# First four tiles of x and two units of weights as one sequence in a fixed order on each engine, with loads in parts and products of ones as TensorE's first work

## The chip, the cores and the metric

The kernel runs on one core of one Trainium2 chip. The metric is device microseconds from one launch to its end; where several executions were timed, the median counts. Each row of the profile comes from one profiled execution, whose own time and span are given below. The core has five engines that run their own instruction streams in order: TensorE (PE, with its weight loads shown apart as PEld), VectorE (DVE), ScalarE (ACT), GpSimd (POOL) and SyncE (SP). SP issues nearly all the DMAs here; in the rows, SPq is its queue.

## What is computed

One layer of an encoder trunk over x (2048 positions, 1024 channels, float32): RMSNorm, one input projection split into ten groups of 1024 columns, a gated linear recurrence in both directions (branch A), a spatial gating unit (branch B), two merge gates, an output projection and a final RMSNorm. Cut to its skeleton:

```python
h = _rmsnorm(x, norm_w[layer])
proj = jnp.einsum('bsd,de->bse', h, w_in[layer])
(q_raw, ffwd_raw, fbwd_raw, i_raw, ga_raw,
 u_raw, v_raw, gb_raw, ma_raw, mb_raw) = jnp.split(proj, split_points, axis=-1)
y_a = _hgrn2_branch(q_raw, ffwd_raw, fbwd_raw, i_raw, ga_raw, lb[layer, 0], lb[layer, 1], gnorm_w[layer])
y_b = _spatial_gating_branch(u_raw, v_raw, gb_raw, ln_w[layer], ln_b[layer], w_s[layer], b_s[layer])
merged = (jax.nn.sigmoid(ma_raw) * jnp.einsum('bsw,wd->bsd', y_a, w_proj_a[layer])
          + jax.nn.sigmoid(mb_raw) * jnp.einsum('bsw,wd->bsd', y_b, w_proj_b[layer]))
x = x + jnp.einsum('bsd,de->bse', merged, w_out[layer])
return _rmsnorm(x, final_norm_w)
```

Only the first line and the first two column groups used (i_raw, here called v, and q_raw) matter for the change.

## The kernel before

Every float32 operand of a projection is kept as two float16 parts, a high one and a low one, and each product is made of three matmuls into one PSUM tile: high by high, high by low, low by high (`mm3`, lines 211 to 218; the rows of lines 215, 216 and 217). The contraction of 1024 is eight steps of 128, so one output tile takes 24 matmuls.

**x.** The 2048 positions are 16 tiles of 128 rows, four to a segment `b`. `x_load` (line 260) fetches a tile of 512 KB into one of three buffers. `x_tile` (line 265) then does the following: ScalarE squares the tile and sums it (line 270); GpSimd makes the reciprocal root in two small instructions (lines 293, 294); for each half `i` of the channels VectorE multiplies by the root and by the norm weights `nwb[i]`, which were broadcast to all partitions by a DMA (line 275); TensorE transposes four blocks into PSUM (line 279); ScalarE writes the high part (line 280) and VectorE the low part (line 281) into `xT[b]`. The scale `sx` of x comes from `scale_x` (line 79): a small DMA of the norm weights, a maximum on VectorE, a transpose and a product on TensorE, and a power of two.

**Weights.** A unit is 1024 rows by 256 columns of `w_in`, 1024 KB. `halves` (line 170) loads it with one DMA (line 177), sums its squares in two pieces on ScalarE (line 182), converts the sums on GpSimd (line 185), adds them over the partitions with two small products on TensorE (line 191), makes a power of two from them (`pow2`, line 126, four VectorE instructions of one column, and line 196), writes the high part in two ScalarE instructions of 1024 columns (line 203) and the low part in one VectorE instruction of 2048 columns (line 204). `load` starts this and gives back a function that ends it; `unit` and `plan` keep the list of units: v, q, and the two forget gates for each pair of heads, 16 units in all, then two wide ones.

**Who decides the order.** A scheduler places the traced instructions on each engine; `tc.high_priority(40)` pulls a block ahead of what is traced before it. `hook(cols, f)` calls `f` in the trace once so many matmul columns have been traced, so that work for a later tile is traced inside the products of an earlier one.

**The start.** `phase1` (line 298) loads the first tile of x, calls `scale_x`, starts the first unit (v) at raised priority, fetches the two halves of `nwb`, and then loops over segments and tiles. After each second tile `v_seg` (line 427) makes v for two tiles of positions: 48 matmuls of 256 columns and one eviction on ScalarE (line 432). After the four tiles of a segment `q_seg` (line 435) makes q of one head: 24 matmuls of 512 columns, then a sigmoid on ScalarE (line 440, with a table load ahead of the first), a product on VectorE (line 444) and a sum of squares on ScalarE (line 445). After segment 3 come `decays` and the recurrence's loop, in which `gla_operands` (line 448), `gla_scores`, `gla_states` and `gla_outputs` work on segments of 512 positions while the projections of the next one run.

## Time and profile before

| what | value |
|---|---|
| median of three timed runs | 2392.24 us (2387.44 to 2392.54) |
| the profiled execution's own time | 2392.29 us |
| its span, first to last instruction | 2390.6 us |
| mean granted TensorE clock | 0.995 |
| TensorE busy | 2322.1 us (97%), 12880 matmuls |
| VectorE, ScalarE, GpSimd busy | 1541.3, 1019.9, 277.3 us |

A row of the timeline gives the start in us, the duration in us, the engine, the line, the operation, the tiles as out<-in with the shape, and how many equal instructions were merged; in brackets stands how long the engine sat idle before it and what released it. A row of the windows gives a stretch, its length, the busy time of TensorE with the number of matmuls, the granted clock, the share of DMA time and GB/s. A matmul's duration includes its way through the array, so in a stream the distance from start to start counts, not the duration. A row of the waits names who waited for whom, the sum in us, the number of times and the longest.

### The profile page before, as it was taken

Reading aid. Unit: us, or ns where it says so; the run is one execution under the profiler, and the core shown is the slowest. Engines: PE = TensorE matmul, PEld = TensorE weight load, DVE = VectorE, ACT = ScalarE, POOL = GpSimd, SP = SyncE. Lnnn points to the kernel's source line nnn. Section 1 sums busy time; section 2 is a strip of 40 time slices with the busy share of each in tenths; the row PEclk is TensorE's granted clock in tenths of the full one; section 3 lists DMA queues with packets and bytes.
Section 4 is the critical chain, followed back from the end, with each engine's and each line's share of the span. In section 5 each row is a group of like instructions: output and inputs, shape, how many; then the busy total and the mean of one; then the engine's idle time right before and its main releaser. Section 6 shows DMA issues by size and latency. Waiting matters only on the chain. (4 is left out here: it accounts for less than half of the span.)

```text
span 2390.6 us, 33841 instructions
## 1 busy us (share of the span) xinstructions
PE 2322.1 (97%) x12880; PEld 1295.7 (54%) x12880; DVE 1541.3 (64%) x3032; ACT 1019.9 (43%) x1870; POOL 277.3 (12%) x507
## 2 busy tenths in 40 slices
PE   7999999999999999999999999999999999999998
PEld 5666866685668566544554554444444444444443
DVE  5686648755773677696555556677665655577754
ACT  6524332433333334333445455656654533244432
POOL 2222202220212121211000000000000000000011
PEclk9999999999999999999999999999999999999999
DMA  5201110011001001122432223666665574777733
GB/s 178 79 6 31 36 36 10 27 36 36 14 23 52 2 14 58 47 62 80 133 101 84 83 86 141 225 248 253 234 219 184 191 274 160 269 238 272 251 117 115
DMA packets 169486, 281.26 MB, mean 118 GB/s; under 512 B 10976, under 2 KB 105184, under 8 KB 162144
## 3 DMA queue, kind: packets, MB, share of 16 engines
q1 hardware_dynamic: 169312, 278.98, 34.4%
q8 instruction: 104, 1.70, 0.3%
q14 instruction: 70, 0.57, 0.1%
HBM read 174.08 MB, written 104.86 MB: 117 GB/s over the span
## 5 line engine op out<-in xcount | busy, mean ns | idle before, releaser
L808 PEld LDWEIGHTS <-seven 128*128 128x128 f16 x5376 | 524.6, 98 | 641.2 <-issue 27.9
L808 PE MATMUL bank<-seven 128*128 128x512 f16 x2016 | 438.3, 379 | 9.1 <-DVE zs L822 7.1
L808 PE MATMUL bank<-xT,seven 128*128 128x512 f16 x1920 | 428.5, 381 | 4.8 <-ACT zs L775 2.4
L808 PE MATMUL bank<-xs,seven 128*128 128x512 f16 x1440 | 319.3, 379 | 0.0
L217 PE MATMUL pin<-xT,wsplit 128*128 128x512 f16 x768 | 291.2, 379 | 0.2 <-DVE wsplit L204 0.2
L215 PE MATMUL pin<-xT,wsplit 128*128 128x512 f16 x768 | 291.1, 379 | 0.2 <-ACT xT L280 0.2
L216 PE MATMUL pin<-xT,wsplit 128*128 128x512 f16 x768 | 291.1, 379 | 0.0
L216 PE MATMUL pin<-wsplit,xT 128*128 128x256 f16 (+1 forms) x768 | 238.2, 310 | 2.7 <-DVE wsplit L204 2.1
L217 PE MATMUL pin<-wsplit,xT 128*128 128x256 f16 (+1 forms) x768 | 238.3, 310 | 2.0 <-DVE xT L281 1.7
L215 PE MATMUL pin<-wsplit,xT 128*128 128x256 f16 (+1 forms) x768 | 238.0, 310 | 0.8 <-ACT xT L280 0.8
L822 DVE SCALAR_TENSOR_TENSOR zs<-bank,us,zs 128x512 f32<-128x512 f32 x120 | 88.9, 745 | 74.1 <-PE bank L808 72.8
L829 ACT ACTIVATE zs<-zs 128x512 f32<-128x512 f32 x120 | 75.2, 627 | 135.0 <-DVE zs L822 134.8
L217 PEld LDWEIGHTS <-wsplit 128*128 128x128 f16 x768 | 75.1, 98 | 90.3 <-DVE wsplit L204 0.7
L700 DVE TENSOR_TENSOR tmp<-raw 128x512 f32<-128x512 f32 x64 | 43.9, 689 | 124.0 <-ACT tmp L685 110.7
L822 DVE SCALAR_TENSOR_TENSOR zs<-bank,su,zs 128x512 f32<-128x512 f32 x72 | 53.8, 747 | 104.3 <-PE bank L808 80.3
L216 PEld LDWEIGHTS <-wsplit 128*128 128x128 f16 x768 | 75.1, 98 | 77.5
L215 PEld LDWEIGHTS <-wsplit 128*128 128x128 f16 x768 | 75.4, 98 | 75.8
L504 POOL TENSOR_TENSOR q<-ff,e 128x512 f32<-128x512 f32 x64 | 73.3, 1145 | 371.8 <-DVE e L502 213.4
L457 ACT ACTIVATE fz<-pin,wus 128x512 f32<-128x512 f32 x64 | 43.9, 685 | 144.3 <-PE pin L217 144.1
L775 ACT ACTIVATE zs<-bank,us 128x512 f32<-128x512 f32 x120 | 80.5, 677 | 50.6 <-PE bank L808 47.6
L217 PEld LDWEIGHTS <-xT 128*128 128x128 f16 x768 | 75.7, 99 | 42.1 <-DVE xT L281 4.6
L461 DVE TENSOR_SCALAR fz<-fz,fb,fa 128x512 f32<-128x512 f32 x64 | 35.6, 556 | 97.2 <-ACT fz L457 97.2
(205 smaller groups left out, 3618.5 us busy)
## 6 DMA issues: line engine op xcount, KB each, us to landing
kept<-seven SPq DMA_DIRECT2D x16, 1792.0 KB, 7.9
seven<-kept SPq DMA_DIRECT2D x16, 1792.0 KB, 9.2
wraw<-in_w_in_dram SPq DMA_DIRECT2D x20, 1024.0 KB, 5.1
raw<-in_w_in_dram SPq DMA_DIRECT2D x40, 512.0 KB, 4.8
xt<-in_x_dram SPq DMA_DIRECT2D x16, 512.0 KB, 4.1
o_d<-ob SPq DMA_DIRECT2D x32, 256.0 KB, 2.3
v<-V SPq DMA_DIRECT2D x16, 512.0 KB, 3.5
vl<-v SPq DMA_DIRECT2D x32, 256.0 KB, 2.9
```

The lines of the kernel that those rows point to most:

```text
L215: nc.tensor.matmul(ps, lh(k), rh(k), start=(k == 0), stop=False)
L216: nc.tensor.matmul(ps, lh(k), rl(k), start=False, stop=False)
L217: nc.tensor.matmul(ps, ll(k), rh(k), start=False, stop=(k == KT - 1))
L457: nc.scalar.activation(out=fz[:, 1:SEG + 1], in_=ps, func=AF.Sigmoid, scale=us)
L461: nc.vector.tensor_scalar(out=f, in0=f, scalar1=fb, scalar2=fa, op0=ALU.mult, op1=ALU.add)
L504: nc.gpsimd.tensor_tensor(out=q0.rearrange("p (m c) -> p m c", c=64), in0=ff.rearrange("p (m c) -> p m c", c=64), in1=e8.rearrange("p n b ...
L700: sub = lambda out, x, y: self.nc.vector.tensor_tensor(out=out, in0=x, in1=y, op=ALU.subtract)
L775: self.nc.scalar.activation(out=t, in_=ps, func=AF.Copy, scale=su)
L808: nc.tensor.matmul(ps, lhs(x, k), rhs(y, k), start=start and not (k or n), stop=k == 3 and n == 2, skip_group_check=True)
L822: self.nc.vector.scalar_tensor_tensor(out=more, in0=ps, scalar=su, in1=more, op0=ALU.mult, op1=ALU.add)
L829: self.nc.scalar.activation(out=out, in_=more, func=func)
```

## The change

`phase1` no longer treats segment 0 in its loop. A new method `start` writes out, as one sequence, everything up to v of all four tiles of segment 0, and the preparation of the q unit. Inside `in_order` each instruction gets an ordering edge to the one traced before it on the same engine, so each engine runs its part in exactly this order; a block `issue_after` puts what follows behind the last of them on each engine, until the constants of `phase1` have been traced.

In `start`:

- TensorE's first work is ten float32 products of `ones` by `ones` (128 by 128) into a PSUM tile that nobody reads; five more stand behind `scale_x`, three behind the first tile's transposes, six behind the sums of the weights' squares: 24 in all (`busy`).
- The first tile of x is the first DMA on SP's queue (before: the second, behind the v unit). The small load of the norm weights in `scale_x` goes to ScalarE's queue. The v unit comes in four DMAs of 256 KB (`part`), two behind each half of `nwb`; the loads of tiles 1, 2 and 3 follow, then the q unit.
- ScalarE squares the first tile of x, then the four parts of the unit. The low part of the unit is made in four VectorE instructions of 512 columns, the high part in four ScalarE instructions of 512 columns; the square of tile 1 stands ahead of the four high parts.
- The high part of the first tile's first half is written by VectorE (`alone=True`), all others by ScalarE.
- Squares, norms, transposes and splits of tiles 1 to 3 are hooked into the 96 products of v at fixed steps. The q unit is begun (`begin`) in the second tile's products and ended (`end`) in the third's.

Outside `start`: `x_tile` is divided into `x_rstd`, `x_norm`, `x_turn` and `x_split`; and `halves` makes the low part of every unit with `w_part`, in two VectorE instructions of half the columns, each behind its own half of the high part, where it was one instruction behind both.

```diff
@@ scale_x
-            nc.sync.dma_start(out=nwt, in_=self.nw.rearrange("(p k) -> p k", k=KT))
+            nc.scalar.dma_start(out=nwt, in_=self.nw.rearrange("(p k) -> p k", k=KT))
@@ halves
             for h in range(2):
-                ks = slice(h * K // 2, (h + 1) * K // 2)
-                nc.scalar.activation(out=wt[:, 0, ks], in_=raw[:, ks], func=AF.Copy, scale=s)
-            nc.vector.scalar_tensor_tensor(out=wt[:, 1].rearrange("p k n -> p (k n)"),
...
+                self.w_part(raw, wt, s, slice(h * K // 2, (h + 1) * K // 2))
+    def w_part(self, raw, wt, s, ks, which=(0, 1)):
+        flat = lambda z: z[:, ks].rearrange("p k n -> p (k n)")
+        if 0 in which:
+            self.nc.scalar.activation(out=wt[:, 0, ks], in_=raw[:, ks], func=AF.Copy, scale=s)
+        if 1 in which:
+            self.nc.vector.scalar_tensor_tensor(out=flat(wt[:, 1]), in0=flat(raw), scalar=s, in1=flat(wt[:, 0]),
+                                                op0=ALU.mult, op1=ALU.subtract)
+    @contextmanager
+    def in_order(self, last):
+        traced = self.nc.cur_bb.bb.instructions
+        old = traced[-1]
+        yield
+        start = next(n for n in reversed(range(len(traced))) if traced[n] is old) + 1
+        for ins in traced[start:]:
+            if ins.engine in last:
+                self.tc.add_manual_dep(ins, last[ins.engine].name, ...)
+            last[ins.engine] = ins
+    def start(self, nwb, last):
...
+            busy(10)
+            x = [self.x_load(0)]
+            self.scale_x()
+            busy(5)
+            for i in range(2):
+                t = self.gat.tile([P, SEG], F32, name="nwb", tag="at")
+                nc.sync.dma_start(out=t, in_=self.nw[i * SEG:(i + 1) * SEG].partition_broadcast(P))
+                nwb.append(t)
+                for ks in part[2 * i:2 * i + 2]:
+                    nc.sync.dma_start(out=raw[:, ks], in_=rows[:, ks])
+            x += [self.x_load(t) for t in range(1, 4)]
+            rstd = self.x_rstd(0, 0, x[0])
+            ss = [sm.tile([P, 2], F32, name="wss") for _ in range(2)]
+            for h, ks in enumerate(part):
+                nc.scalar.activation(out=wt[:, 1, ks], in_=raw[:, ks], func=AF.Square, accum_out=ss[h // 2][:, h % 2:h % 2 + 1])
+            sb = [sm.tile([P, 2], BF16, name="wsb") for _ in range(2)]
+            for h in range(2):
+                nc.gpsimd.tensor_copy(out=sb[h], in_=ss[h])
+            for i in range(2):
+                self.x_norm(x[0], rstd, nwb, i)
+            pt = [self.x_turn(0, i, x[0]) for i in range(2)]
+            busy(3)
+            self.x_split(0, 0, 0, pt[0], True)
+            pb = self.pg.tile([P, 1], F32, name="misc")
+            for h in range(4):
+                nc.tensor.matmul(pb, self.ones16, sb[h // 2][:, h % 2:h % 2 + 1], start=(h == 0), stop=(h == 3))
+            busy(6)
...
+            self.pow2(s, inv, pb)
...
+            self.x_split(0, 0, 1, pt[1])
+            rstd = {1: self.x_rstd(0, 1, x[1])}
+            wi, got = (wt, us), {}
+            for h in range(2):
+                self.w_part(raw, wt, s, part[h])
+            for h in range(2):
+                self.w_part(raw, wt, s, part[2 + h], (0,))
...
+            square(2)
+            for i in range(2):
+                norm(1, i)
+                self.w_part(raw, wt, s, part[2 + i], (1,))
+            for t, k, f in ((0, 4, partial(split, 1, 0)), (0, 6, partial(split, 1, 1)), (0, 6, partial(square, 3)),
+                            (0, 8, partial(norm, 2, 0)), (0, 8, partial(norm, 2, 1)),
+                            (1, 4, partial(split, 2, 0)), (1, 6, partial(split, 2, 1)), (1, 6, begin),
+                            (1, 8, partial(norm, 3, 0)), (1, 8, partial(norm, 3, 1)),
+                            (2, 4, partial(split, 3, 0)), (2, 6, partial(split, 3, 1)), (2, 7, end)):
+                self.hook((8 * t + k) * 3 * U, f)
+            v = self.v_seg(0, *wi, range(1))
+            v = self.v_seg(0, *wi, range(1, 2), v)
+        return wi, got["q"], v
@@ phase1
-                first = [self.x_load(0)]
-                self.scale_x()
-                with tc.high_priority(40):
-                    wi = self.load(*self.todo[0])
...
-                for b in range(NSEG):
+                last = {}
+                with tc.high_priority(60):
+                    wi, wq, vt[0] = self.start(nwb, last)
+                behind = ExitStack()
+                for ins in last.values():
+                    behind.enter_context(tc.issue_after(ins))
+                qs[0] = self.q_seg(0, 0, 0, *wq)
+                for b in range(1, NSEG):
                     for j in range(4):
-                        self.x_tile(b, j, nwb, first.pop() if first else self.x_load(4 * b + j))
-                        if j == 1 and b == 0:
...
-                        elif j % 2:
+                        self.x_tile(b, j, nwb, self.x_load(4 * b + j))
+                        if j % 2:
                             vt[b] = self.v_seg(b, *wi, range(j // 2, j // 2 + 1), vt[b])
```

As built, ScalarE's order around the q unit also differs. Before, it ran: the two squares of the third unit (a forget gate's), first eviction of v, high parts of tile 3, high parts of the q unit, squares of tiles 4, 5 and 6, second eviction of v, table load, sigmoid of q, high parts of tile 4. Now it runs: first eviction of v, high parts of tile 3, high parts of the q unit, second eviction of v, squares of tiles 4, 5 and 6, the two squares of the third unit, table load, sigmoid of q, high parts of tile 4. On SP's queue the third unit's load stands behind two more tiles of x than before. From the recurrence's loop on, the order on TensorE, ScalarE, GpSimd and SyncE is the same but for short runs of a few instructions that stand a few places earlier or later; VectorE has the second low half of each unit in addition.

## The prediction

> **What bounds the kernel now.** I read the page first, then TensorE by stretches, then the timeline of the first 40 us, then who waits for whom.

> ```profile
> span 2390.6 us, 33841 instructions
> PE 2322.1 (97%) x12880; PEld 1295.7 (54%) x12880; DVE 1541.3 (64%) x3032; ACT 1019.9 (43%) x1870; POOL 277.3 (12%) x507
> ```
> ```profile
> 0.00:14.00 14.00, 3.19 (x14) 1.00 0.87 289
> 14.00:31.00 17.00, 15.47 (x123) 1.00 0.62 196
> 31.00:60.00 29.00, 27.81 (x202) 1.00 0.34 114
> 60.00:105.00 45.00, 42.50 (x305) 0.96 0.23 80
> 105.00:960.00 855.00, 845.71 (x5601) 1.00 0.09 28
> ```

> TensorE sets the end: it is idle for 68.5 us of 2390.6. Of these, 10.8 lie before 14 us, 1.5 in 14 to 31, 1.2 in 31 to 60, 2.5 in 60 to 105 and 9.3 in 105 to 960. The change rewrites what happens before 31 us, so at most some 12 us of idle time are there to be had, 0.5% of the whole. Busy time hides a second loss:

> ```profile
> 13.87 0.39 PE L215 MATMUL pin<-wsplit,xT 128*128 128x256 f16 x1
> 15.50 0.37 PE L216 MATMUL pin<-wsplit,xT 128*128 128x256 f16 x1 [1.24 <-DVE wsplit L204]
> ...
> 16.36 0.42 PE L215 MATMUL pin<-wsplit,xT 128*128 128x256 f16 x1
> 16.57 0.42 PE L216 MATMUL pin<-wsplit,xT 128*128 128x256 f16 x1
> ...
> 20.35 0.27 PE L217 MATMUL pin<-wsplit,xT 128*128 128x256 f16 x1
> 20.46 0.27 PE L215 MATMUL pin<-wsplit,xT 128*128 128x256 f16 x1
> ```

> The first real matmul starts at 13.87 and the second at 15.50. At 16.4 two starts lie 0.21 apart, at 20.4 0.11: TensorE runs at half pace up to about 19.8, over some 17 matmuls, which costs 1.8 us. The clock also falls later:

> ```profile
> 67.60:71.00 3.40, 1.80 (x13) 1.00 0.60 239
> 71.00:74.40 3.40, 3.40 (x19) 0.50 0.00 0
> ```

> A stretch with 1.6 us idle of 3.4 is followed by 3.4 us at half clock, a loss of 1.7.

> **The change part by part.** *Loads.* These rows give the landings:

> ```profile
> 2.38 1.14 SPq L320 DMA_DIRECT2D nwb<-in_norm_w_dram  x2
> 6.51 1.06 ACT L182 ACTIVATE wsplit<-wraw 128x1024 f16<-128x1024 f32 x1 [4.44 <-DMA wraw<-in_w_in_dram]
> 7.98 0.16 DVE L88 TENSOR_REDUCE am<-nwt 128x1 f32<-128x8 f32 x1 [6.78 <-DMA nwt<-in_norm_w_dram]
> ```
> ```profile
> DMA to landing us min/median/max: 7.0/7.2/7.3
> ```

> The unit's 1024 KB land at 6.5; x's 512 KB and the tiny load behind them by 8.0. So 512 KB take 1.5, the unit 3.0, and data flow from 3.5. The last row is `nwb`'s: issued at 2.4 and 3.0, landed at 9.4 and 10.3, so 256 KB of broadcast take 0.9 to 1.4; I use 1.2. A quarter of a unit is bounded by half of an x tile, 0.75, and by a broadcast, 1.4; its rows are read once from memory as x's are, so 0.75. In the new order x lands at 5.0, the first `nwb` at 6.2, parts at 6.95 and 7.7, the second `nwb` at 8.9, parts at 9.65 and 10.4, tile 1 at 11.9. The tiny load, first on ScalarE's queue, is wanted for `sx` by 9.6 only, and landed at 8.0 as the third in line. Tile 3 needs tile 0's buffer (free at 10.1), and the q unit stands behind it on SP; landings of a unit:

> ```profile
> DMA to landing us min/median/max: 5.7/6.5/11.0
> ```

> The q unit, issued at 10.6, lands by 21.6 at the latest, and its squares' turn is at 21.8. The third unit stands behind tiles 4 and 5, whose buffers come free with the transposes at 17 and 21: issued at 21.7, landed by 32.7, wanted at 33.7. Both are hidden, by little at the longest row; GpSimd's constants, now behind the sequence, are wanted from 105 on.

> [...] The broadcast rows, 256 KB each and 0.9 to 1.4 apart, show no fixed cost that adds up in a queue. With one, the sum would be that of the last rival below.

> *From the loads to the first product.* Prices:

> ```profile
> 10.11 0.16 DVE L130 TENSOR_SCALAR p2t<-misc 128x1 f32<-128x1 f32 x1
> 10.58 0.56 POOL L294 TENSOR_TENSOR rstd<-xss,mhalf 128x1 f32<-128x1 f32 x1
> 10.88 2.19 ACT L203 ACTIVATE wsplit<-wraw,ws 128x1024 f16<-128x1024 f32 x2 [1.14 <-DVE ws L135]
> 11.17 1.42 DVE L275 SCALAR_TENSOR_TENSOR xt<-xt,rstd,nwb 128x512 f32<-128x512 f32 x2 [0.27 <-POOL rstd L294]
> 13.10 2.35 DVE L204 SCALAR_TENSOR_TENSOR wsplit<-wraw,ws,wsplit 128x2048 f16<-128x2048 f32 x1 [0.52 <-ACT wsplit L203]
> 13.98 0.69 ACT L280 ACTIVATE xT<-xps,sx 128x512 f16<-128x512 f32 x1 [0.17 <-PE xps L279]
> ```

> Sums to scale take 0.77 (10.11 to 10.88). Operations of 512 columns are 0.7 on VectorE (two in 1.42) and, by half of 1.06 and of 2.19/2 plus 0.15 fixed, 0.65 (square) and 0.7 (high part) on ScalarE. The last part lands at 10.4: square and its sum to 11.2, conversion and two products to 11.6, scale at 12.4. x's own chain is shorter: root at 7.1 (square 1.05 and 0.2, GpSimd 0.8), first norm and transposes behind it, second norm when `nwb` is there, 9.6, transposed at 10.1. ScalarE does that half's high part to 11.9 and, in the fixed order, tile 1's square (landed 11.9, 1.05 and 0.1) to 13.05. Only then comes the first high part of the weights: first product at 13.8, the low part 0.75 later: second at 14.5. That is 0.1 and 1.0 earlier than now. VectorE then steps through low part, norm, low part, norm, low part, 0.67 each, to 17.9; TensorE keeps pace, and ends tile 0 at 18.55. Left are 72 products at 0.109 (7.85), 16 transposes at 0.109 (1.75) and about 0.8 of short waits for tiles 2 and 3: v ends at 29.0.

> ```profile
> 30.88 0.38 PE L215 MATMUL pin<-xT,wsplit 128*128 128x512 f16 x1
> ...
> 31.66 0.39 PE L217 MATMUL pin<-xT,wsplit 128*128 128x512 f16 x1 [0.19 <-DVE wsplit L204]
> ...
> 36.42 1.91 PE L279 MATMUL xps<-ident,xt 128*128 128x128 f32 x16
> ...
> 38.83 0.28 PE L217 MATMUL pin<-wsplit,xT 128*128 128x256 f16 x1
> ```

> Now it ends at 30.9: **1.9 won**. That includes the products of ones. Their price is bounded by the float32 products of the recurrence:

> ```profile
> 114.94 0.92 PE L570 MATMUL pu<-vt,ks 128*128 128x128 f32 x6
> ```

> Six entries are three products, 0.25 each, 0.5 at half pace. Ten and five from 1.0 on fill TensorE to some 7.4; three (0.75) end by 10.7 behind the transposes; six from 11.6 end at 13.1, or 14.6 at half pace, where they would hold up the first product by 0.8. I take full pace.

> *The q unit and the hand-over.* VectorE is through with tile 3 at 26.9, scale at 27.7, first high half at 28.9, its low half (half of 2.35 and 0.1) at 30.2. q starts at 29.0, waits 0.75 at its third product, and 22 more at 0.216 end it at 35.0 (now 36.4): 1.4 left. Then ScalarE decides:

> ```profile
> 27.02 2.20 ACT L203 ACTIVATE wsplit<-wraw,ws 128x1024 f16<-128x1024 f32 x2
> ...
> 32.93 1.28 ACT L440 ACT_TABLE_LOAD   x1
> 36.62 0.69 ACT L440 ACTIVATE qsig<-pin,wus 128x512 f32<-128x512 f32 x1 [2.41 <-PE pin L217]
> 37.21 1.25 ACT L280 ACTIVATE xT<-xps,sx 128x512 f16<-128x512 f32 x2
> ```

> Today it is idle for 2.41 ahead of the sigmoid. In the new order its queue is: high halves to 29.95, eviction 30.55, three squares at 1.04 to 33.7, the third unit's two squares to 35.75 (now done at 23.2, in the gap that the faster start removes), table load 37.05, sigmoid 37.7, tile 4's high part 38.4. TensorE ends its 16 transposes at 36.7 and waits 1.7; with VectorE's q product and low part behind the sigmoid it resumes at 39.2, against 38.83 with two transposes fewer done: **lead 1.9 becomes a lag of 0.1**. Behind it the third unit's scaling now falls into segment 1, in place of segment 2 with its 1.6 idle at 67.6 to 71; I put the idle time of 39 to 105 at 0.4 more.

> *Low parts in halves*, all other units:

> ```profile
> DVE wsplit L204 <- ACT wsplit L203: 24.9, 11, 2.6
> ```
> ```profile
> PE sc L531 <- DVE ff L488: 3.1, 3, 1.0
> PE po L593 <- DVE fend L475: 2.2, 1, 2.2
> PE pk L529 <- DVE e L501: 1.2, 1, 1.2
> ```

> In 105 to 960 VectorE stood 24.9 us ahead of 11 low parts until ScalarE had both high halves. Behind one half it starts 1.1 earlier each time (half of 2.19), 12 us in all, less 0.2 a unit for the second instruction. Of this TensorE can get between nothing and its 9.3 idle there, of which 6.5 waited for VectorE in these rows. The units' low parts stand ahead of only a part of those waits: I take 0.3 for each of 11, **3.0 won**.

> Sum: 0.1 + 0.4 - 3.0 = -2.5 against the execution's own 2392.3, which is the median of the runs (2392.24): **2389.8**. A half-clock stretch costs the same wherever it falls, so I leave it.

> **The rivals.** *The lead is kept.* If the third unit's squares slip behind the sigmoid's work or the waits fill with other transposes, 1.4 stays, the stretch at 71 goes (1.7), the halves give 3.0: 2392.3 - 6.1 = 2386.2. For it: 2.41 of ScalarE's slack; against: its fixed queue. *Slower: TensorE's gaps at the hand-overs halve the clock.* Place: 36.7 to 38.4, and again where the third unit's low part stands in front of tile 6's. It decides from 1.6 us idle in 3.4, as at 67.6; I have 1.7 here. Two stretches at 1.7 on the lag of 0.5, with VectorE's gain lost in other waits: 2392.3 + 3.9 = 2396.2. [...] *It does nothing.* The start is hidden by the hand-over, and VectorE's time goes into its own later waits: +0.5, 2392.8. *Each part pays a start of its own.* A lone x tile lands in 3.3 at best:

> ```profile
> DMA to landing us min/median/max: 3.3/4.3/8.8
> ```

> That is 1.8 over its 1.5 of data; three more starts put 5.4 on the first product, and 0.1 + 5.4 + 0.4 - 3.0 makes 2395.2. Broadcasts 0.9 to 1.4 apart speak against it.

> **How the numbers follow.** Forecast 0.42, lead kept 0.27, clock 0.13, nothing 0.14, parts 0.04. What cannot be told from no change is about 0.2%, 4.8 us: faster is below 2387.5, slower above 2397.0. Faster: 0.24 of the lead kept, and a quarter of the forecast, 0.11: 0.35. Slower: half the clock case and the upper ends of the last two, 0.11. Within: 0.54. The range reaches from 2385.0, a little past the lead kept, to 2395.5, short of the clock case.

> **What would show it.** Right: second product near 14.5, starts 0.11 apart from then on, q's first product near 29.0, a wait of TensorE of about 1.7 near 37 to 38.5 for tile 4's high part, resumption near 39.2; waits of VectorE for the high parts about 12 us shorter. Wrong: starts 0.21 apart behind 14 us, or the second product behind 15.5 (loads or clock); no gap at 37 (lead kept); half clock behind the hand-overs; idle time in 105 to 960 still 9.3 (halves worth nothing).

## The result, and the profile after

| what | before | after |
|---|---|---|
| median of ten timed runs each | 2387.96 us | 2395.34 us (2392.13 to 2397.05) |
| ratio after to before, 95% interval | | 1.0022 (1.0014 to 1.0031) |
| the profiled execution's own time | 2392.29 us | 2393.87 us |

The change makes the kernel slower by 0.22%, 5.3 us (0.0022 times 2388). The two medians of ten lie further apart, 7.4 us or 0.31%, at the upper end of that interval; the text goes by the ratio. The two profiled executions hide this: that of before lies 4.3 above its kernel's median of ten, that of after 1.5 below.

The page of the changed kernel, first its span and busy times, then two rows of its costliest groups (busy, mean ns of one, idle time ahead of them and what ended most of it):

```profile
span 2392.1 us, 33980 instructions
...
PE 2327.3 (97%) x12930; PEld 1298.3 (54%) x12930; DVE 1552.2 (65%) x3055; ACT 1020.6 (43%) x1875; POOL 267.6 (11%) x508
```
```profile
L221 PE MATMUL pin<-wsplit,xT 128*128 128x256 f16 (+1 forms) x768 | 237.6, 309 | 7.5 <-PEq L1001 4.2
L220 PE MATMUL pin<-wsplit,xT 128*128 128x256 f16 (+1 forms) x768 | 237.8, 310 | 5.1 <-issue 3.2
```

TensorE is still what ends the run. New are the two releasers at the right: 4.2 us behind TensorE's own sequencer (PEq) at line 1001, and 3.2 for which the profile names nothing ("issue"). Line 1001 (887 in before) is `with tc.If(flag > 0)`, the branch to the exact path, 960 us behind the new start. Lines 219 to 221 of the changed kernel are the three products of `mm3`, lines 215 to 217 of before. TensorE by stretches, after and then before (start and end, length, busy time, matmuls, granted clock, DMA share, GB/s):

```profile
31.00:60.00 29.00, 25.67 (x190) 1.00 0.34 110
...
105.00:960.00 855.00, 846.90 (x5606) 1.00 0.09 28
...
990.00:1012.00 22.00, 14.60 (x60) 0.84 0.22 61
```
```profile
990.00:1012.00 22.00, 21.60 (x101) 1.00 0.23 65
```

In 990 to 1012 TensorE does 60 products where it did 101. Products stand 0.213 to 0.216 us apart there, so the 41 missing ones are 8.8 us. TensorE's timeline around the branch, after, then before; line 1479 (1365 in before) is the product in `range_flag` that counts the partitions whose values are within range, and the flag made from it is what the branch tests:

```profile
995.28 0.19 PE L1479 MATMUL cnt<-ones,fmin 128*1 128x1 f32 x2
995.40 0.39 PE L219 MATMUL pin<-wsplit,xT 128*128 128x512 f16 x1
995.63 0.38 PE L220 MATMUL pin<-wsplit,xT 128*128 128x512 f16 x1
1000.23 0.38 PE L221 MATMUL pin<-wsplit,xT 128*128 128x512 f16 x1 [4.22 <-PEq L1001]
1000.44 0.38 PE L219 MATMUL pin<-wsplit,xT 128*128 128x512 f16 x1
1004.00 0.58 PE L220 MATMUL pin<-wsplit,xT 128*128 128x512 f16 x1 [3.18 <-issue]
1004.38 0.63 PE L221 MATMUL pin<-wsplit,xT 128*128 128x512 f16 x1
1004.80 0.63 PE L219 MATMUL pin<-wsplit,xT 128*128 128x512 f16 x1
```
```profile
982.80 0.19 PE L1365 MATMUL cnt<-ones,fmin 128*1 128x1 f32 x2
...
999.82 0.38 PE L217 MATMUL pin<-wsplit,xT 128*128 128x512 f16 x1
1000.59 0.38 PE L216 MATMUL pin<-wsplit,xT 128*128 128x512 f16 x1 [0.40 <-PEq L887]
```

Three things are lost: 4.22 at the branch against 0.40; 3.18 two products behind it; and from then to 1007.7 starts 0.43 apart, at half clock. In the built order of before, the count product stands 74 products ahead of the branch; in the changed kernel three. No edited line asks for that; the scheduler decided it. The text ahead of the prediction calls the two orders the same there but for instructions that stand a few places earlier or later; this product moved by 71 products.

### The profile page after: what moved, and what is told of

Read it like the earlier page. It is cut to its first block, busy times and chain, and to the rows that moved or that the text cites. A ratio compares the mean times of both kernels' runs of the same rounds, so it can differ in the third digit from the quotient of the medians.

```text
span 2392.1 us, 33980 instructions
## 1 busy us (share of the span) xinstructions
PE 2327.3 (97%) x12930; PEld 1298.3 (54%) x12930; DVE 1552.2 (65%) x3055; ACT 1020.6 (43%) x1875; POOL 267.6 (11%) x508
```

## The experiments

Each kernel was timed in five rounds against the kernel before on the same chip; ratios are to before, with 95% intervals of about 0.1% (2.3 us) to each side. The gaps are those of one profiled execution: the first at the branch, the second behind it. "Ahead" is the number of products between the count product and the branch in the built order. "Place" is the number, in the program's list of TensorE instructions (an fp32 product counted as four), of the first instruction of the code that runs behind the branch.

| kernel | ahead | place | first gap | second gap | ratio |
|---|---|---|---|---|---|
| before | 74 | 30049 | 0.4 | none | 1 |
| after | 3 | 30146 | 4.2 | 3.2 | 1.0022 (1.0014 to 1.0031) |
| e1 before, count late | 3 | 30053 | 4.0 | none | 1.0029 (1.0015 to 1.0044) |
| e2 before, halves | 3 | 30047 | 3.8 | none | 1.0027 (1.0017 to 1.0036) |
| e3 after, whole low parts | 74 | 30149 | 0.4 | 3.0 | 1.0019 (1.0008 to 1.0031) |
| e4 after, count early | 60 | 30142 | 0.2 | 2.2 | 1.0002 (0.9993 to 1.0010) |
| e5 as e4, code moved | 60 | 30158 | 0.4 | none | 0.9982 (0.9973 to 0.9991) |
| e6 before, code moved | 74 | 30145 | 0.5 | 2.3 | 1.0001 (0.9992 to 1.0011) |
| e7 after, code moved | 3 | 30162 | 4.1 | none | 1.0013 (1.0004 to 1.0022) |
| e8 as e3, code moved | 74 | 30165 | 0.4 | none | 0.9991 (0.9981 to 1.0001) |
| e9 as e5, hand-over | 60 | 30155 | 0.3 | none | 0.9986 (0.9977 to 0.9994) |
| e10 before, halves, count early | 60 | 30043 | 0.2 | none | 0.9998 (0.9989 to 1.0007) |
| e11 as e4, no products of ones | 60 | 30046 | under 0.3 | none | 1.0016 (1.0007 to 1.0025) |
| e12 as e5, count 14 ahead | 14 | 30158 | 1.8 | none | 0.9985 (0.9975 to 0.9995) |

**e1: the count product alone.**

```diff
+            mms = [i for i in nc.cur_bb.bb.instructions if isinstance(i, mybir.InstMatmult)]
+            with tc.issue_after(mms[-4]):
-            nc.tensor.matmul(pc, fm, self.ones[:, 0:1], start=True, stop=True)
+                nc.tensor.matmul(pc, fm, self.ones[:, 0:1], start=True, stop=True)
```

> The kernel before with one move: the product that counts the range flag, 74 products ahead of the branch on TensorE in the kernel before, is held back until three products ahead of it, as in the changed kernel. Theory A (the place of the count product costs the time): TensorE's queue is empty when it branches, so at the branch a gap of about 4 us and one of about 3 us behind it, in place of 0.4; with half a clock behind the gaps some 8 to 10 us in all, so 2396 to 2398 against 2388. Rival B (the start, its fixed order and its waits cost the time): 2388, no change. Rival C (the halves' extra instructions cost it behind the branch): 2388. Rival D (the loss at the branch comes from the changed kernel's other instruction addresses, not from the order): two short gaps at most, 2388.

Measured: 2395.27 us, ratio 1.0029, a little below the 2396 to 2398 told. TensorE's waits in 990 to 1012 of this kernel (who waits for whom, sum, times, longest):

```profile
PE pin L215 <- PEq L887: 4.0, 1, 4.0
```

One instruction moved, with nothing else of the change, costs as much as the change. Theory A held for this gap; the second one, which A also wanted here, did not come. So the second gap needs something that this kernel lacks.

**e2: the halves alone.**

```diff
-                ks = slice(h * K // 2, (h + 1) * K // 2)
-                nc.scalar.activation(out=wt[:, 0, ks], in_=raw[:, ks], func=AF.Copy, scale=s)
-            nc.vector.scalar_tensor_tensor(out=wt[:, 1].rearrange("p k n -> p (k n)"),
...
+                self.w_part(raw, wt, s, slice(h * K // 2, (h + 1) * K // 2))
```

> The kernel before with the low parts of every unit in two halves and nothing else of the change. The scheduler then puts the count product three products ahead of the branch by itself. Theory A: 8 to 10 us lost at the branch, 2 to 3 won ahead of it by the halves: 2394 to 2396, slower than before by 0.25 to 0.35%. Rival B (the start costs the time): 2385 to 2388. Rival C (the halves' instructions cost it): slower too, 2393, but the lag against the kernel before would grow over the later stretch from 1010 us on and not stand at the branch.

Measured: 1.0027, within the 0.25 to 0.35% told; first gap 3.8, no second. The halving of the low parts is enough to make the scheduler move the count product. The new start is not: in e3 and e8, which have it without the halves, the product keeps its place. Why the scheduler answers so was not looked into.

**e3: the change with whole low parts.**

```diff
-                self.w_part(raw, wt, s, slice(h * K // 2, (h + 1) * K // 2))
+                self.w_part(raw, wt, s, slice(h * K // 2, (h + 1) * K // 2), (0,))
+            self.w_part(raw, wt, s, slice(0, K), (1,))
```

> The changed kernel with the low part of every unit whole again, all else of the change kept (the start's order, loads in parts, products of ones). The count product then stands 74 products ahead of the branch again. Theory A: no drained queue at the branch; the start's gain of 1 to 2 us is left: 2386 to 2388 (ratio to before 0.9990 to 1.0000). Rival B: still slower, 2393 or more. Rival C: 2388 or less, but the difference to the changed kernel spread over the stretch behind 1010 us.

Measured: 1.0019, a miss for theory A, which wanted 2386 to 2388. The waits in 990 to 1012:

```profile
PE pin L222 <- issue: 3.0, 1, 3.0
PE pin L221 <- PEq L1002: 0.4, 1, 0.4
```

The first gap went as told. The second stayed, and here it has no drained queue ahead of it: it belongs to the new start, or to what the start does to the program.

**e4: the change with the count product early.**

```diff
+        with tc.high_priority(60):
             fm = sm.tile([P, 1], F32, name="fmin")
```

> The changed kernel with one move: the count product is given an earlier place, 60 products ahead of the branch in place of three; all else of TensorE's order stays. Theory A: the gaps of 4.2 and 3.2 us at the branch go, and with them the half clock behind them: 2395.3 less 8 to 10 is 2385 to 2387, faster than before by 0.05 to 0.15% and the first of these kernels to be so. Rivals B and C: 2395, no change against the changed kernel.

The edit raises the flag's whole chain, its reductions on VectorE included. Measured: 2388.12 us, 1.0002, where 2385 to 2387 was told: most of the loss is gone, but not all, since the second gap stayed.

```profile
PE pin L220 <- issue: 2.2, 1, 2.2
PE pin L219 <- PEq L1001: 0.2, 1, 0.2
```

Where the second gap stands gave the next theory. TensorE stopped after four products in e4, after two in the changed kernel, after one in e3. A product here is two instructions, a weight load and the matmul (the page of the changed kernel counts 12930 of each); with the places of the table, 30142 + 8, 30146 + 4 and 30149 + 2 are 30150, 30150 and 30151: the same place of the code. The 24 products of ones are fp32, 96 instructions, and moved all later code by that much.

Theory E, to be tried by the runs, is that TensorE stops at this place of the code, whatever ran ahead of the branch, because a second piece of code has to be fetched there; the expectations call it a piece's end. In e5 the code behind the branch begins past it, at 30158: by E the second gap goes, and the half clock behind it, and 2384 to 2385 us (0.9982 to 0.9990) are left. In e6, in which nothing that runs is changed, it begins five or six instructions ahead of it, at 30145.

**e5 to e8: the code moved, nothing else.** In the arm that is not taken, products of ones are added that never run:

```diff
+            pad = pin.tile([P, P], F32, name="pad", tag="pin")
+            for _ in range(4):       # 24 in e6
+                nc.tensor.matmul(pad, self.ones, self.ones, start=True, stop=True)
             for hp in range(H // 2):
                 wi, ui = self.load(self.w_in, C_I + U * hp)()
```

> The changed kernel with the count product 60 products ahead of the branch, and four fp32 products of ones (16 instructions of TensorE) at the head of the arm that is not taken; they never run and only move the place of the code behind the branch by 16 instructions. [...] Rival F (the second gap is a wait that the new start causes, a buffer or a transfer, not a matter of addresses): gap and time stay, 2388. Rival G (any instruction added moves this by chance): no gap to be told in advance.

> [...] Theory E: TensorE stops for 2 to 3.5 us after about two products behind the branch (the address predicts two or three), half a clock behind it: 4 to 5 us, 2392 to 2393 (ratio 1.0016 to 1.0022). Rivals F and G: 2388, no second gap.

> The changed kernel with four fp32 products of ones in the arm that is not taken, the count product where the change has it. Theory E with theory A: the second gap (3.2 us) goes, the first (4 us, TensorE's queue drained at the branch) stays: 2395.3 less 4 to 5 is 2390.5 to 2391.5. Rival F: 2395.

> The changed kernel with whole low parts (so the count product 74 products ahead) and four fp32 products of ones in the arm that is not taken: what is left of the change that runs is the new start alone, without either gap at the branch. Theories A and E: 2392.4 less 4 to 5 is 2387.5 to 2388.5, no change against the kernel before, since the profile so far shows the start's lead of 1.5 us at 32 us spent by 105 us. If the start were worth what the prediction says (nothing but its lag of 0.1 us): 2388. Rival F: 2392.

Measured, e5: no second gap (its only wait in 990 to 1012 follows), and 2385.35 us, 0.9982: faster than the kernel before, with the whole change in it.

```profile
PE pin L219 <- PEq L1001: 0.4, 1, 0.4
```

The timeline of e6, the kernel before with 96 dead instructions:

```profile
997.38 0.38 PE L216 MATMUL pin<-wsplit,xT 128*128 128x512 f16 x1 [0.52 <-PEq L887]
997.59 0.38 PE L217 MATMUL pin<-wsplit,xT 128*128 128x512 f16 x1
997.81 0.38 PE L215 MATMUL pin<-wsplit,xT 128*128 128x512 f16 x1
1000.50 0.39 PE L216 MATMUL pin<-wsplit,xT 128*128 128x512 f16 x1 [2.32 <-issue]
```

Three products, six instructions behind 30145: 30151 again. Rivals F and G are out; the new start waits for nothing there. Rival D of e1, which blamed the addresses, was wrong about the first gap and right about the second. But the time of e6 was a miss: 1.0001, where 1.0016 to 1.0022 was told. Its gap cost no half clock (see the last section), and 2.3 us, 0.1%, is as wide as the interval. e7 keeps its first gap alone (4.1) at 1.0013, e8 has neither, at 0.9991.

The traces point to a fetch of code, though no row of TensorE names one. In 990 to 1006 an instruction queue moves packets (count, MB, share of 16 engines; the view does not say which engine it feeds), in the changed kernel, in before and in e5:

```profile
q8 instruction: 3, 0.05, 1.8%
```
```profile
q8 instruction: 3, 0.05, 1.4%
```
```profile
q8 instruction: 2, 0.03, 0.8%
```

Three packets in 0.05 MB are some 16 KB each; on the page of either kernel the whole run has 104 in 1.70 MB. The count does not tell the kernels apart, but the packets' times in the traces do. In each of these kernels one packet moves while the branch instruction runs, and the next starts 0.5 to 1.1 us after TensorE's first product behind the branch. In the changed kernel that second packet moves from 1000.72 to 1002.65, and TensorE resumes at 1004.00; in e6 from 997.88 to 999.07, and TensorE resumes at 1000.50. In e3 and e4 too the resumption comes 1.4 to 1.6 us behind the packet's end. In before (1001.10 to 1002.36) and in e5 (996.70 to 997.79) the second packet moves beside running products. TensorE resumes 3.8 us after its first product behind the branch in the changed kernel (1000.23 to 1004.00) and 3.1 in e6 (997.38 to 1000.50), whether it did two products or three in between. Where the code behind the branch begins some 50 products ahead of that place, as in before (30049; an estimate from the places, half of 30150 less 30049), TensorE comes to it 10.7 us behind the branch (50 at 0.214), near 1011.3, when the second packet has been over since 1002.36. That TensorE stands at that place for the second packet is the author's estimate from these times: the rows have "issue" for the stop, and the 1.4 to 1.6 us from the packet's end to the resumption are not accounted for. The runs do not show how many instructions a piece has, since all four stops (after, e3, e4, e6) are one place.

**e9: the hand-over at 38 us.**

```diff
                     for j in range(4):
-                        self.x_tile(b, j, nwb, self.x_load(4 * b + j))
+                        with tc.high_priority(20 if b == 1 and j == 0 else 0):
+                            self.x_tile(b, j, nwb, self.x_load(4 * b + j))
```

> The kernel of e5 with a higher priority for the first tile behind the start (tile 4), so that on ScalarE its two high parts stand between and ahead of the third unit's squares and ahead of the table load of q's sigmoid, in place of behind all of them. Theory H (the hand-over stall that the prediction priced at 1.7 us is what eats the start's lead): TensorE's wait of 1.4 us at 38 us for tile 4's high part falls below 0.5, and the lead at 105 us rises by 0.7 to 1.4 us; the time 2384 to 2385 where e5 has 2385 to 2386 (ratio to before 0.9976 to 0.9982). Rival: the wait moves to the low part or to the next tile (1.9 us at 50 us), and nothing is won.

Measured: 0.9986, no better than e5. ScalarE did write tile 4's high parts at 34.88 and 36.61, ahead of the table load, and TensorE then waited for VectorE in place of ScalarE:

```profile
38.58 0.28 PE L221 MATMUL pin<-wsplit,xT 128*128 128x256 f16 x1 [1.35 <-DVE xT L296]
```

In e5 it resumed at 38.59, behind 1.40 for the high part. The rival was right: the wait moved to the low part and kept its length. The lead at 105 us, told to rise, fell: TensorE is idle for 4.2 us in 60 to 105 where it was 2.4 in e5.

**e10: halves without the start, e11: the start without products of ones.** e10 is e2 with e4's edit; e11 is e4 with the four `busy` calls out.

> The kernel before with the low parts in halves and the count product given its place 60 products ahead of the branch; no new start. The code behind the branch begins where a piece lasts 50 products, so neither gap at the branch. Theories A and E: what is left is the halves alone: TensorE leads by about 2 us (e2: 3.4 at 900 us, of which 1.4 are a stretch of half clock at 71 us in the profile of before) to 3 us (the prediction's figure) ahead of the branch: 2385.5 to 2387 on a chip where before has 2388.2 (ratio 0.9988 to 0.9993). If halves were what costs the time behind the branch (rival C): 1.0010 or more.

> The changed kernel without the 24 products of ones, count product 60 ahead, no gap expected from the place of the code (50 products to the piece's end). The first products run at half clock again, from 13.4 to about 17 or 20 us: each of some 20 to 30 costs 0.1 us more: 2 to 3 us lost against e5 by 31 us. If all of that reaches the end: ratio 0.9990 to 0.9996; if the products of ones are worth nothing: 0.9982 as e5.

Measured, e10: 0.9998, where 0.9988 to 0.9993 was told; its interval reaches down to 0.9989. The halves cost nothing behind the branch (rival C is out), and what they gain is too small for five rounds. e11: 1.0016, more than any theory had. Its first products:

```profile
13.43 0.37 PE L219 MATMUL pin<-wsplit,xT 128*128 128x256 f16 x1 [1.87 <-ACT wsplit L210]
...
16.30 0.42 PE L221 MATMUL pin<-wsplit,xT 128*128 128x256 f16 x1
...
17.37 0.29 PE L219 MATMUL pin<-wsplit,xT 128*128 128x256 f16 x1
```

They stand 0.21 apart to 16.5 and 0.11 from 17.4 on. That, and one stretch of half clock at 51.5, put it 3.6 us behind e5 by 105 us (lead -2.7 against 0.9, table below). The ratios say 0.34%, 8 us, with some 3 to each side. By the mean granted clock of all timed runs (0.9958, in e5 0.9966) some 2 us of this would be half clock, an estimate; the rest was not found.

**e12: fourteen products ahead.** e5 with 20 in place of 60 in `tc.high_priority`.

> The kernel of e5 with the count product 14 products ahead of the branch in place of 60. Theory A in numbers: from the count product to the first product behind the branch the changed kernel takes 5.3 us (994.97 to 1000.23), the work of 24 or 25 products at 0.213 us; 14 products cover 3.0 of it, so a gap of 2.0 to 2.5 us at the branch, in place of 0.4 with 60 and 4.2 with three; with half a clock behind it 3 to 4 us in all: ratio 0.9994 to 0.9999. A rival, by which only a count product that is last in the queue costs anything: gap 0.4, ratio 0.9982.

The chain of the expectation begins one product early: the count product itself starts at 995.28, so from it to the first product behind the branch are 4.95 us. Measured:

```profile
992.74 0.19 PE L1481 MATMUL cnt<-ones,fmin 128*1 128x1 f32 x2
...
995.47 0.38 PE L221 MATMUL pin<-wsplit,xT 128*128 128x512 f16 x1
997.67 0.38 PE L219 MATMUL pin<-wsplit,xT 128*128 128x512 f16 x1 [1.83 <-PEq L1001]
```

From 992.74 to 997.67 are 4.93 us: the chain of count, comparison on VectorE, load of the flag and branch took 4.95 and 4.93 in the two kernels. In these runs, whatever of it the products behind the count do not cover is idle: 4.2 with three, 1.8 with fourteen, 0.2 to 0.4 with sixty. The rival is out by the gap. The time, 0.9985, is below what was told, and in the profiled execution the half clock did not come; by the time alone e12 cannot be told from e5.

## Why the prediction was wrong, point by point

**The start was right almost to the row, up to 39 us.** First product told 13.8, second 14.5, pace 0.11, q's first product 29.0, its third product 0.75 late, q done at 35.0, and a wait of 1.7 at the hand-over with TensorE back at 39.2. Measured:

```profile
13.44 0.27 PE L219 MATMUL pin<-wsplit,xT 128*128 128x256 f16 x1 [0.43 <-ACT wsplit L210]
14.23 0.27 PE L220 MATMUL pin<-wsplit,xT 128*128 128x256 f16 x1 [0.52 <-DVE wsplit L212]
14.34 0.27 PE L221 MATMUL pin<-wsplit,xT 128*128 128x256 f16 x1
...
28.89 0.39 PE L219 MATMUL pin<-xT,wsplit 128*128 128x512 f16 x1
...
30.21 0.39 PE L221 MATMUL pin<-xT,wsplit 128*128 128x512 f16 x1 [0.72 <-DVE wsplit L212]
...
34.97 1.91 PE L285 MATMUL xps<-ident,xt 128*128 128x128 f32 x16
38.27 0.28 PE L219 MATMUL pin<-wsplit,xT 128*128 128x256 f16 x1 [1.40 <-ACT xT L295]
```

The products come up to 0.4 earlier than told, and TensorE is back 0.9 earlier; in 31 to 60 it is idle for 3.3 us (29.00 less 25.67) against 1.2. The wait is the one told, for the reason told: on ScalarE the third unit's second square (34.50), then the table load and the sigmoid, then tile 4's high parts:

```profile
34.50 1.05 ACT L182 ACTIVATE wsplit<-wraw 128x1024 f16<-128x1024 f32 x1
...
35.66 1.28 ACT L554 ACT_TABLE_LOAD   x1
36.95 0.69 ACT L554 ACTIVATE qsig<-pin,wus 128x512 f32<-128x512 f32 x1
37.54 1.26 ACT L295 ACTIVATE xT<-xps,sx 128x512 f16<-128x512 f32 x2
```

**The lead into the branch was right in sum, by luck.** The next table is worked out from the traces: the same instruction of ScalarE or VectorE (line text and number) is looked up in two traces, and the median over all of a stretch says by how many us the kernel leads the profiled execution of before.

| kernel | 105 to 200 us | 900 to 950 us | 1200 to 1300 us |
|---|---|---|---|
| after | 1.3 | 2.5 | -5.3 |
| e1 before, count late | 1.5 | 1.4 | -3.2 |
| e2 before, halves | 2.0 | 3.4 | -0.9 |
| e3 after, whole low parts | 0.2 | 0.2 | -4.4 |
| e4 after, count early | 0.9 | 2.2 | -0.7 |
| e5 as e4, code moved | 0.9 | 2.1 | 3.2 |
| e6 before, code moved | 2.1 | 2.1 | 1.0 |
| e7 after, code moved | 1.0 | 2.3 | -1.5 |
| e8 start alone, code moved | 0.1 | 0.1 | 0.3 |
| e9 as e5, hand-over | -0.4 | 0.7 | 2.4 |
| e10 before, halves, count early | 1.3 | 2.6 | 4.6 |
| e11 no products of ones | -2.7 | -1.4 | 0.7 |
| e12 as e5, count 14 ahead | 0.9 | 2.2 | -1.0 |

e1 and e6 run the same code as before in the first two stretches and lead by 1.4 to 2.1: that is the stretch of half clock at 71 us, which they do not have. The third column holds further such stretches, two of before at 951.7 and 965.3 and none to two of the others there, and is no measure of what a kernel gains. Against e1 and e6 the start alone (e3, e8) is 1.3 to 2 behind at 105, where the prediction had 0.1 + 0.4. Part of this is the 0.4 for 39 to 105: TensorE's waits there add up to 3.8 and 4.1 us in e3 and e8, 4.3 in the changed kernel and 3.2 in before. In 105 to 960, the stretch that the prediction worked on, the *halves* are worth the rise from the first column to the second: 1.1 to 1.4 in every kernel that has them, 0.0 or -0.1 in those that do not. The prediction's **"3.0 won"** for them (its 0.3 for each of 11 would be 3.3) was over twice too much there. So the 2.5 that the changed kernel leads by at 900 us is the 2.5 of the sum by other terms: it lacks the stretch at 71 (1.7), which the sum left in and which e1 and e6 lack too with the old code there, and it got less from the start and from the halves. VectorE did wait less for the high parts, as told (14.0 us against 24.9, told "12 us in all"):

```profile
DVE wsplit L212 <- ACT wsplit L210: 14.0, 11, 1.5
```

and TensorE got little of it: 8.1 idle in 105 to 960 (855 less 846.90) against 9.3. It found a new wait:

```profile
PE pk L643 <- DVE df L595: 2.7, 1, 2.7
```

**The step that failed** is "Low parts in halves": besides the size, it counted what VectorE's second instruction does to the waits of 105 to 960, and took the order behind that for unchanged. The prediction says "The change rewrites what happens before 31 us"; the halves rewrite every unit, the two wide ones ahead of the branch too, and there the scheduler answered by moving the range count from 74 products ahead of the branch to three. On the two orders side by side this looks like one small product a little later. Which engine waits on it, and how long its chain is, was not asked. Its price is shown by e1 (+0.29%), by e7 against e5 (0.31% more) and by after against e4 (0.20%): 5 to 7 us.

The second failed term is one the prediction did not have: the length of the program. 24 products of ones were priced by their time on TensorE (nothing, as they fill idle time), not by the 96 instructions by which they move the code behind the branch. Price, by e4 against e5 0.20%, e3 against e8 0.28%, after against e7 0.09%, e6 against before 0.01%: 3 to 4 us on average, each with some 3 us of uncertainty.

"**A half-clock stretch costs the same wherever it falls, so I leave it**" failed with them. In these traces a stretch follows idle time (last section). The profiled execution of the change lost the one at 71 and has a double one behind the branch.

**The sum.** Told was -2.5 us, 0.10%. That 2395.34 lies just inside the stated 2385.0 to 2395.5 is luck: the forecast stood on an execution 4.3 us above before's median of ten, and the loss is none of its terms. With both losses at the branch taken away and all else of the change kept, e5 measures -0.18% (-0.27 to -0.09), 4.3 us. So the sum of the part that the prediction worked out lies within what e5 measures, though not its split, and what it did not look at outweighed it twice over. Of the rivals, "slower by half clock at the hand-overs" had the sign, not the place. What stays open is how e5's 4.3 us divide: by the leads the start loses 1.3 to 2 (e8 against e1 and e6) and the halves win 2.0 on top of it (e5 against e8 at 900 us), about nothing in sum, while by the timed runs e8, the start alone, is at 0.9991, not at 1.0006, and e11 is 4 us slower than its lead says. Half clock does not explain e5's gain: its mean granted clock over all timed runs is 0.9966, that of the runs of before beside it 0.9968. These differences are about as large as the intervals.

**A version that beats both.** e5 is faster than the kernel before by 0.18%, and by the two ratios 0.4% faster than the changed one; its relatives e9 and e12 are at 0.9986 and 0.9985, which the intervals do not tell from it.

## What to carry to other kernels

Where a scheduler decides, compare the order along the whole program, and for each instruction that moved ask what branch or register load waits on its result: ahead of the branch here the count of covering products mattered (by an estimate 23 of 0.213 us for the chain of 4.9; 3, 14, 60 and 74 were run), and a priority on the flag's chain bought them (e4 against after, 0.20%). Added instructions moved the code behind the branch, so when a time changes far behind an edit, look just behind the next taken branch for a stop that no semaphore explains (3.18 us in the changed kernel); dead instructions in an arm that is not taken moved the code without running and showed it in one run (96 in e6, a gap of 2.32; 16 in e5, none).

## What the runs showed of the hardware

In these runs a branch whose flag came in time left TensorE idle for 0.2 to 0.5 us (first gaps with 60 and 74 products ahead): in the trace of before the branch instruction starts at 996.76 and takes 3.67 us, the products issued ahead of it run on to 1000.19, and 0.40 are idle. With three products ahead the same instruction is bare: in the changed kernel it starts at 996.29 and takes 3.77 us, the last product ahead of it ends at 996.01, and the next starts at 1000.23.

```profile
994.05:997.46 3.41, 1.96 (x11) 1.00 0.06 14
997.46:1000.88 3.42, 0.59 (x2) 1.00 0.05 10
1000.88:1004.29 3.41, 0.29 (x1) 0.50 0.01 5
1004.29:1007.71 3.42, 3.42 (x9) 0.50 0.27 75
```
```profile
996.73:1000.14 3.41, 1.22 (x7) 1.00 0.02 5
1000.14:1003.56 3.42, 3.42 (x10) 0.50 0.61 173
```
```profile
995.46:998.88 3.42, 2.20 (x10) 1.00 0.02 5
998.88:1002.29 3.41, 1.79 (x9) 1.00 0.02 5
1002.29:1005.70 3.41, 3.41 (x18) 1.00 0.76 212
```

Behind 0.59 us busy the changed kernel was at half clock for two windows, behind 1.22 e4 for one; behind 2.20 and 1.79 e6 stayed at full clock. Other windows of this length that were followed by half clock had 0.37, 1.35, 1.54 and 1.82 us busy in before (from 1528.50, 948.25, 961.90 and 67.61), 0.69, 1.08 and 1.04 in the changed kernel (from 946.27, 1533.35 and 2113.62) and 1.56 in e11 (from 48.11). Others that were followed by full clock had 1.54 and 1.93 in before (from 1487.56 and 1511.45), 1.83, 1.88 and 1.96 in the changed kernel (from 7.60, 48.56 and 994.05) and 1.67 in e12 (from 994.18). Between 1.54 and 1.83 both were seen, so the prediction's "It decides from 1.6 us idle in 3.4" does not hold of these traces: the 1.54 from 1487.56 left 1.87 idle, and the clock stayed.

The same gap of 2.2 to 2.3 us went with 1.7 more in e4 (half of 3.42), where it fell into one window, and with nothing more in e6, where it fell across two. In these two runs a gap's price followed its place among the windows, which the edits did not control.
